# Stored weight sums of a two-layer encoder, made by HBM copies and adding transfers instead of VectorE

## The chip, the cores and the metric

The kernel runs on one core of a Trainium2 chip. The core has a matrix engine (TensorE, PE in the profile; PEld is its weight load), a vector engine (VectorE, DVE), an activation engine (ScalarE, ACT), GpSimd (POOL) and SyncE (SP), each with its own queue of instructions that it works off in order. Transfers between HBM and on-chip memory (SBUF) run on 16 DMA engines. SP, ACT and GpSimd can issue them, and only GpSimd's can add to what lies at the destination. The metric is the time of one execution in microseconds (us); lower is better. Before the change the median of three runs is 2393.16 us (2392.74 to 2401.15).

## What is computed

256 tokens of width 2048 pass two layers. Each is a norm, a token mixer (a bidirectional mLSTM in layer 0, a bidirectional HGRN2 in layer 1), a residual addition, a second norm, and a gated feed-forward part with a short convolution, again with a residual addition. A norm closes the trunk. All of it is float32. Cut to what matters here:

```python
for layer in range(DEPTH):                       # 2
    hn = rmsnorm(h, norm_mix_g[layer])
    h = h + (mlstm_mixer if layer % 2 == 0 else hgrn_mixer)(hn, ...)
    h = h + conv_glu(rmsnorm(h, norm_ffn_g[layer]), ...)
return rmsnorm(h, final_g)

def conv_glu(hn, w_up, conv_w, conv_b, w_down):  # w_up 2048 x 11008, w_down 5504 x 2048
    a, v = jnp.split(hn @ w_up, 2, axis=-1)
    c = conv_b + <width-3 convolution of a over the tokens>
    return (jax.nn.gelu(c, approximate=False) * v) @ w_down
```

Nearly all of the work is the matrix products with weights that are read from HBM once, some 440 MB.

## The kernel before

**Products.** A float32 operand is split into a rounded part and the rest (xh + xl, wh + wl), and a product is taken from three of the four parts. Weights come in pieces of 128 x 2048 (1 MB, tile raw, loaded by line 130 or, in the up-projection, line 368); ACT rounds 1024 columns to wh (line 142), VectorE subtracts to wl (line 143), TensorE multiplies (lines 330 and 334, 346, 229). A chunk is one stretch of such products with its own PSUM banks; `stream` takes the chunks of the whole program in order.

**Stages.** mLSTM until 389 us; feed-forward of layer 0: 22 up chunks (389 to 637), down products (637 to 749), 21 up chunks (749 to 982), down products (982 to 1095); HGRN until 1678; the feed-forward of layer 1 in the same four steps until the end.

**Seven products instead of eight.** In the down products two blocks of 128 rows (of both the activations and the weights) form a couple, a 2 x 2 block product. For some couples (SEVEN, 22 in a layer, in three chunks of kind "st": 8, 8 and 6) seven block products are taken instead of eight, Winograd's form. They need four sums of the couple's weight blocks B11, B22, B21, B12, called T1 to T4. These 44 couples' sums depend on weights alone, and the kernel keeps them in an HBM buffer, tscr. `split_squares` loads them later as if they were weights (T<-tscr, raw<-tscr).

**Who makes the sums.** The generator `prepare`, once for each half of a layer's feed-forward: it loads a couple's 1 MB into two tiles pwh and pwl (two loads of 512 KB, SP's queue, line 368), makes four VectorE subtractions of 128 x 512 (line 598), and stores both tiles to tscr (line 601, SP's queue). It does so while the up chunks run.

**What sets the order.** The program is written as one stream of TensorE work; other work is given to `side` as generators that yield an estimated delay, and `side.tick` advances them. The tile framework (`schedule_with_timeline_sim=True`) then reorders the instructions of each engine by what they depend on and by its own estimate of durations; only instructions given to `tc.keep_in_program_order` (`pin`, `late`) keep their place. Transfers of HWDGE queues (SP, ACT) take turns on eight counters and GpSimd's on eight others; one that takes a counter waits for the transfer that used it last. Several small results go through GpSimd in the first mixer: rc (line 421), the square root of the first norm's mean square, by which all that leaves the first projection is scaled; the broadcasts Mb (line 764), which the heads' weights need; and rs (line 506), which scales a head's output y before TensorE transposes it (pz, line 821).

Of the kernel before, what the change touches and what calls it, by code (L numbers as in the profile page):

```python
# [8 lines left out]
F32 = mybir.dt.float32  # L9
# [3 lines left out]
ALU = mybir.AluOpType  # L13
PSUM = bass.MemoryType.PSUM

P = 128
T = 256
# [27 lines left out]
MORE = 2  # L45
MIX = 5
LEAD = 48
TEMP = 3
GATES = 4 * AH
SEVEN = (1, 2, 3, 4, 6, 7, 8, 9), (1, 2, 4, 5, 7, 8)  # L50
# [10 lines left out]
def trunk_kernel(ctx, tc, xT, x_d, fg_d, pp_d, cst_d, w_gate, w_first, w_aq, w_ak, w_av, w_ao, w_aout, w_ao2,  # L61
# [467 lines left out]
    def token_sums(mp, i, a, b, S, last=None):  # L529

        m = 384 if last else 512
        sx = mp.tile([P, 2 * m], F32R, tag=f"sx{i}", name="sx")
        for i, (x, y, op) in enumerate(((a[:, P:T], b[:, P:T], ALU.add), (a[:, P:T], a[:, 0:P], ALU.subtract),
                                        (S[:, 0:P], a[:, 0:P], ALU.subtract), (b[:, 0:P], S[:, 2 * P:3 * P], ALU.subtract))):
            dve.tensor_tensor(S[:, i * P:(i + 1) * P], x, y, op)
        act.copy(sx[:, 0:m], S[:, 0:m])
        dve.tensor_tensor(sx[:, m:2 * m], S[:, 0:m], sx[:, 0:m].bitcast(F32), ALU.subtract)
        if last:
            act.copy(last[0], S[:, m:512])
            dve.tensor_tensor(last[1], S[:, m:512], last[0].bitcast(F32), ALU.subtract)  # L540
        return [(sx[:, i * P:(i + 1) * P], sx[:, m + i * P:m + (i + 1) * P]) for i in range(m // P)] + ([last] if last else [])

    def pair(src, nk, c0, x, sums, norm, seven):

        def part(t, c):
            o = 512 * (c0 + c)
            return hm[:, t, o:o + 512]

        def mid(ps):
# [6 lines left out]
            dve.tensor_tensor(part(0, 1), part(0, 1), u, ALU.add)  # L556
            dve.tensor_tensor(part(1, 1), part(1, 1), P5, ALU.add)
            dve.tensor_tensor(u, u, P7, ALU.add)  # L558
            pool.tensor_tensor(part(1, 0), part(1, 0), u, ALU.add)  # L559
            pool.tensor_tensor(part(1, 1), part(1, 1), u, ALU.add)  # L560

        def done(ps):
            for i in range(4):
# [12 lines left out]
        ch.stored, ch.waits, ch.pool = {}, None, None  # L576
        return ch

    def prepare(mp, todo, period, finished):

        loaded = []

        def load(i):
            if i < len(todo):
                n = ("wh", "wl")[i % 2]
                r = [mp.tile([P, 1024], F32, tag=n, bufs=MORE, name=f"p{n}") for _ in range(2)]
                for j in range(2):
                    late(r[j], todo[i][0][:, j * 1024:(j + 1) * 1024])
                loaded.append(r)

        yield 18.0
        load(0)
        for i, (_, dst) in enumerate(todo):
            yield period / 2
            load(i + 1)
            B11, B22, B21, B12 = (loaded[i][j // 2][:, j % 2 * 512:(j % 2 + 1) * 512] for j in range(4))
            for x, y, out in ((B12, B22, B22), (B12, B11, B12), (B11, B22, B11), (B21, B11, B21)):
                dve.tensor_tensor(out, x, y, ALU.subtract)  # L598
# [515 lines left out]
    def ffn(layer, norm, nxt):  # L1114
        stack = ExitStack()
        box = dict(n=(2 * len(SEVEN[0]) + len(SEVEN[1])) * layer)
        chunks, pairs = [], []

        def begin():
            box["mp"] = stack.enter_context(tc.tile_pool(name="ff", bufs=1))  # L1120
# [36 lines left out]
            return go  # L1157

        for part, (f0, nf) in enumerate(((0, FA), (FA, FB))):
            GT, SX, todo, finished = [], {}, [], []  # L1160

            def prep(todo=todo, finished=finished, nf=nf):
                if not pairs[0].pool:
                    begin()
                side.push(prepare(box["mp"], todo, (nf * 10.4 - 26.0) / len(todo), finished))

            for i in range(nf):
                chunks.append(Chunk("fm", w_up[layer, f0 + i], KT, norm.x, done_up(f0 + i, i, GT, SX, SEVEN[part]),
                                    prep if i == 0 else None,
                                    swap=(2,) if part and i == 0 else (3,) if f0 + i == 1 else (), paced=True))  # L1170
            def two(src, c0, norm, seven, GT=GT, SX=SX, nf=nf, todo=todo, finished=finished):
                ch = pair(src, nf, c0, lambda k: GT[k], lambda u: SX[u], norm, seven)
                for u in seven:
                    ch.stored[u] = tscr[box["n"]]
                    todo.append((src[:, 2048 * u:2048 * (u + 1)], tscr[box["n"]]))
                    box["n"] += 1
                ch.waits, ch.pool = finished, None
                pairs.append(ch)
                return ch

# [18 lines left out]
    n0, n1, n2, n3 = Norm("mix_g", 0), Norm("ffn_g", 0), Norm("mix_g", KT), Norm("ffn_g", KT)  # L1199
    nf = FinalNorm()  # L1200
    chunks = mlstm(n0, n1)
    c, close0 = ffn(0, n1, n2)
    chunks += c
    c = hgrn(n2, n3)
    b = c[0].before
# [2 lines left out]
        close0()  # L1208
        b()
    c[0].before = swap  # L1210
    chunks += c
    c, close1 = ffn(1, n3, nf)
    chunks += c
    stream(chunks)
    close1()

# [98 lines left out]
```

## Time and profile before

| | before |
|---|---|
| runs, median of 3 | 2393.16 us |
| span of the profiled execution | 2388.1 us |
| TensorE busy | 2371.3 us, 99% |
| VectorE busy | 1939.6 us, 81% |
| ScalarE busy | 1352.4 us, 57% |
| GpSimd busy | 189.7 us, 8% |
| moved by DMA | 578.15 MB, 242 GB/s mean |
| mean DMA share, mixers / first up chunks of a layer | 0.50 to 0.67 / 0.89 |

The runs' times are measured around the execution; the span is from the first to the last instruction of one profiled execution and lies 5 us below the median. TensorE's matmuls are pipelined, so that their recorded lengths overlap: a matmul of 512 columns has a record of 0.39 us, while four follow one another in 1.07 us. The DMA share is the mean busy share of the 16 DMA engines. An engine's idle time only costs something where another waits for it, so the list of who waited for whom stands above the busy shares.

### The profile page before, as it was taken

How to read it: one execution, taken by the hardware profiler on the slowest of the kernel's cores; microseconds unless marked ns; L12 is line 12 of the kernel's file. 1: busy time of each engine (PE TensorE's matmuls, PEld its weight loads, DVE VectorE, ACT ScalarE, POOL GpSimd, SP SyncE). 2: the span in 40 equal slices, each digit the busy share in tenths (PEclk: the TensorE clock that was granted, in tenths of full speed). 3: DMA queues.
4: the chain of work that ended last, by engine and by line, in shares of the span. 5: the costliest groups of instructions: out<-in, count | busy, mean ns of one | idle time of the engine just before them, and what ended most of it. 6: DMA issues, size and time to landing. Idle time of an engine off the chain costs nothing.

```text
span 2388.1 us, 38126 instructions
## 1 busy us (share of the span) xinstructions
PE 2371.3 (99%) x14596; PEld 2027.1 (85%) x14596; DVE 1939.6 (81%) x3167; ACT 1352.4 (57%) x2141; POOL 189.7 (8%) x240
## 2 busy tenths in 40 slices
PE   9999999999999999999999999999999999999998
PEld 7888888888788888888888888888888878888887
DVE  7766687888888888767888989889788888888874
ACT  7655455555565555655555555556555566455563
POOL 0100000000000000001222222220000000000000
PEclk9999999999999999999999999999999999999999
DMA  8654546998987777755544554545798998777774
GB/s 301 201 183 163 185 184 226 324 322 323 330 340 277 271 247 242 277 190 182 177 162 175 177 175 164 175 173 190 277 324 326 333 359 310 265 244 249 246 273 143
DMA packets 105703, 578.15 MB, mean 242 GB/s; under 512 B 11936, under 2 KB 12448, under 8 KB 58672
## 3 DMA queue, kind: packets, MB, share of 16 engines
q1 hardware_dynamic: 103824, 571.71, 67.5%
q0 software_dynamic: 1120, 3.21, 0.7%
q8 instruction: 114, 1.87, 0.3%
q10 hardware_dynamic: 576, 0.79, 0.1%
q14 instruction: 69, 0.57, 0.1%
HBM read 527.37 MB, written 48.30 MB: 241 GB/s over the span
## 4 chain that ended last, share of the span: by engine, by line
PE 90%; DMA 6%; DVE 3%; issue 1%; ACT 0%; SPq 0%; POOLq 0%; POOL 0%; DVEq 0%; ACTq 0%
PE mm L330 32%; PE mm L346 23%; PE mm L334 16%; PE pc L229 10%; PE mm L229 5%; DMA pwl<-in_w_d 2%; DVE wl L143 1%; DMA T<-tscr 1%; DMA pwh<-in_w_d 1%; PE pn L793 1%; PE py L1051 1%; DMA tscr<-pwl 1%; PE pd L1001 0%; PE pz L407 0%; PE pa L1001 0%
## 5 line engine op out<-in xcount | busy, mean ns | idle before, releaser
L330 PE MATMUL mm<-xt,wh 128*128 128x512 f32 x3776 | 1314.0, 394 | 0.0
L143 DVE TENSOR_TENSOR wl<-raw,wh 128x1024 fp32r<-128x1024 f32 (+1 forms) x846 | 1033.4, 1227 | 268.7 <-ACT wh L142 265.3
L142 ACT CAST wh<-raw 128x1024 fp32r<-128x1024 f32 (+1 forms) x846 | 874.4, 1040 | 567.1 <-PE mm L330 265.6
L334 PE MATMUL mm<-xt,wl 128*128 128x256 f32 x3776 | 1046.6, 278 | 1.1 <-DVE wl L143 1.1
L330 PEld LDWEIGHTS mm<-xt,wh 128*128 128x128 f32 x3776 | 706.2, 188 | 159.3
L334 PEld LDWEIGHTS mm<-xt,wl 128*128 128x128 f32 x3776 | 709.5, 188 | 6.5 <-DVE wl L143 2.0
L346 PE MATMUL mm<-wh,xt 128*128 128x512 f32 x1024 | 320.6, 391 | 1.8 <-ACT xt L352 1.3
L346 PEld LDWEIGHTS mm<-wh,xt 128*128 128x128 f32 x1024 | 191.5, 188 | 42.0 <-ACT xt L352 1.7
L346 PE MATMUL mm<-wl,xt 128*128 128x512 f32 x512 | 198.2, 391 | 0.0
L229 PE MATMUL pc<-wh,g 128*128 128x512 f32 x576 | 195.1, 390 | 0.3 <-ACT wh L142 0.2
L229 PEld LDWEIGHTS pc<-wh,g 128*128 128x128 f32 x576 | 108.0, 188 | 24.8 <-ACT wh L142 2.0
L229 PE MATMUL pc<-wl,g 128*128 128x512 f32 x288 | 112.3, 390 | 0.9 <-DVE wl L143 0.9
L346 PEld LDWEIGHTS mm<-wl,xt 128*128 128x128 f32 x512 | 96.2, 188 | 18.9
L143 DVE TENSOR_TENSOR wl<-T,wh 128x1024 fp32r<-128x1024 f32 (+1 forms) x100 | 93.8, 951 | 21.7 <-ACT wh L142 21.3
L229 PE MATMUL mm<-wh,sx 128*128 128x512 f32 x300 | 107.1, 391 | 2.8 <-ACT wh L142 2.8
L142 ACT CAST wh<-T 128x1024 fp32r<-128x1024 f32 (+1 forms) x100 | 82.3, 835 | 45.7 <-PE pc L229 23.3
L559 POOL TENSOR_TENSOR hm<-hm,u 128x512 f32<-128x512 f32 x8 | 11.2, 1399 | 1151.6 <-DVE u L558 1151.6
L1138 ACT ACTIVATE avc<-avc,pp 128x256 f32<-128x256 f32 x86 | 51.6, 600 | 87.7 <-DVE avc L1136 87.7
L346 PE MATMUL mm<-wh,g 128*128 128x512 f32 x308 | 96.5, 392 | 0.0
L1133 ACT COPY avc<-mm 128x256 f32<-128x256 f32 x172 | 63.7, 371 | 51.4 <-PE mm L334 50.9
L598 DVE TENSOR_TENSOR pwl<-pwl 128x512 f32<-128x512 f32 x88 | 60.2, 684 | 27.9 <-DMA pwl<-in_w_d 27.9
L598 DVE TENSOR_TENSOR pwh<-pwh 128x512 f32<-128x512 f32 x88 | 60.2, 684 | 27.8 <-DMA pwh<-in_w_d 21.6
(256 smaller groups left out, 2504.3 us busy)
## 6 DMA issues: line engine op xcount, KB each, us to landing
raw<-in_w_up SPq DMA_DIRECT2D x172, 1024.0 KB, 6.1
raw<-in_w_bq SPq DMA_DIRECT2D x48, 1024.0 KB, 4.9
raw<-in_w_d SPq DMA_DIRECT2D x40, 1024.0 KB, 5.2
raw<-in_w_d SPq DMA_DIRECT2D x44, 768.0 KB, 6.7
T<-tscr SPq DMA_DIRECT2D x44, 768.0 KB, 8.0
raw<-in_w_ao SPq DMA_DIRECT2D x24, 1024.0 KB, 4.6
pwh<-in_w_d SPq DMA_DIRECT2D x44, 512.0 KB, 8.1
pwl<-in_w_d SPq DMA_DIRECT2D x44, 512.0 KB, 7.7
```

The costliest lines, as they stand in the source:

```text
L142: pin(act.copy(wh[:, :m], r))
L143: pin(dve.tensor_tensor(wl[:, :m], r, wh[:, :m].bitcast(F32), ALU.subtract))
L229: pe.matmul(ps, a, b, start=id(ps) not in begun, stop=stop and i == 2)
L330: pe.matmul(ps[f], wh[:, c:c + P], x, start=k + kk == 0, stop=False)
L334: pe.matmul(ps[f][:, 0:T], wl[:, c:c + P], x[:, 0:T], start=False, stop=k + kk == ch.nk - 1)
L346: pe.matmul(ps[t], x[:, a + t * P:a + (t + 1) * P], w[:, c], start=st and i == 0, stop=sp and i == 2)
L559: pool.tensor_tensor(part(1, 0), part(1, 0), u, ALU.add)
L598: dve.tensor_tensor(out, x, y, ALU.subtract)
L793: pe.matmul(pn[:, 0:258], w, v, start=(i == 0), stop=(i == len(parts) - 1))
L1051: pe.matmul(py[:, c], AT[:, s if s == t else 2 + s], V[:, s, j * P:(j + 1) * P], start=(s == 0), stop=(s == 1))
L1133: act.copy(z, p[:, T:2 * T])
L1138: act.activation(c, a, AF.Identity, bias=col("conv_b", layer * FT + f), scale=cw[1])
```

## The change

`prepare` makes the sums without SBUF and without VectorE. For each of the 44 couples it copies the couple's four blocks from the weights to tscr (1 MB, HBM to HBM, ACT's queue), and then adds in place by four GpSimd transfers of 128 x 512 each: B12 onto the copy of B22 (T3), B11 onto the copy of B12 (T1), T3 onto the copy of B11 (T2), T2 onto the copy of B21 (T4). An adding transfer can't subtract, so the sums become additions, and the signs move to the activations' sums and to the results' combination. `prepare` of a layer now starts before the third chunk of layer 0's mixer and the second chunk of layer 1's, with an estimated 24 us for each couple; before, it started with the first up chunk of each half. Neither the copies nor the adding transfers are pinned to the program's order.

```diff
+PERIOD = 24.0
...
             for x, y, out in ((B12, B22, T3), (B12, B11, B12), (B22, B12, T2), (B21, T2, T4)):
-                dve.tensor_tensor(out, x, y, ALU.subtract)
+                dve.tensor_tensor(out, x, y, ALU.add)
...
-    def prepare(mp, todo, period, finished):
-        loaded = []
-        def load(i):
-            if i < len(todo):
-                n = ("wh", "wl")[i % 2]
-                r = [mp.tile([P, 1024], F32, tag=n, bufs=MORE, name=f"p{n}") for _ in range(2)]
-                for j in range(2):
-                    late(r[j], todo[i][0][:, j * 1024:(j + 1) * 1024])
-                loaded.append(r)
-        yield 18.0
-        load(0)
-        for i, (_, dst) in enumerate(todo):
-            yield period / 2
-            load(i + 1)
-            B11, B22, B21, B12 = (loaded[i][j // 2][:, j % 2 * 512:(j % 2 + 1) * 512] for j in range(4))
-            for x, y, out in ((B12, B22, B22), (B12, B11, B12), (B11, B22, B11), (B21, B11, B21)):
-                dve.tensor_tensor(out, x, y, ALU.subtract)
-                yield period / 8
-            for j in range(2):
-                nc.sync.dma_start(dst[:, j * 1024:(j + 1) * 1024], loaded[i][j])
-        finished.append(True)
+    def prepare(todo, period):
+        for src, dst, last in todo:
+            nc.scalar.dma_start(dst, src)
+            yield period / 4
+            T2, T3, T4, T1 = (dst[:, j * 512:(j + 1) * 512] for j in range(4))
+            B11, B22, B21, B12 = (src[:, j * 512:(j + 1) * 512] for j in range(4))
+            pool.dma_start(T3, B12, accum_op=ALU.add)
+            pool.dma_start(T1, B11, accum_op=ALU.add)
+            yield period / 4
+            pool.dma_start(T2, T3, accum_op=ALU.add)
+            yield period / 4
+            pool.dma_start(T4, T2, accum_op=ALU.add)
+            if last is not None:
+                last.append(True)
+            yield period / 4
...
-        return chunks, stack.close
+        return chunks, stack.close, lambda: side.push(prepare(todo, PERIOD))
...
-    c, close0 = ffn(0, n1, n2)
+    c, close0, chunks[2].before = ffn(0, n1, n2)
...
-    c, close1 = ffn(1, n3, nf)
-    chunks += c
+    d, close1, c[1].before = ffn(1, n3, nf)
+    chunks += c + d
```

Where the instructions stand after the framework's reordering, on the two engines that issue the new transfers. First GpSimd's queue in the first mixer, before the change (from the casts of a constant to the second broadcasts):

```order
L691 CAST Vh<-pad 128x2x2 x2
L691 CAST Vl<-pad 128x2x2 x2
L421 ISA
L421 TENSOR_TENSOR rc<-rc,mhalf 128x2
L717 MEMSET B 64x256
L733 DMA mscr<-M 64x256
L764 DMA Mb<-mscr 128x256 x12
L506 TENSOR_TENSOR rs<-rs,mhalf 128x2 x2
L764 DMA Mb<-mscr 128x256 x4
```

With the change, around rc (lines 587, 588, 590 and 592 are the four adding transfers, T3, T1, T2 and T4; rc is now line 422, B line 710):

```order
L588 DMA tscr<-in_w_d 128x512
L422 ISA
L422 TENSOR_TENSOR rc<-rc,mhalf 128x2
L587 DMA tscr<-in_w_d 128x512
L588 DMA tscr<-in_w_d 128x512
L590 DMA tscr<-tscr 128x512
L587 DMA tscr<-in_w_d 128x512
L588 DMA tscr<-in_w_d 128x512
L710 MEMSET B 64x256
```

Sixty-six adding transfers stand ahead of rc, where before none did. And further down, around the last adding transfers (the broadcasts Mb are now line 757, rs line 507):

```order
L590 DMA tscr<-tscr 128x512 x8
L592 DMA tscr<-tscr 128x512
L590 DMA tscr<-tscr 128x512 x2
L592 DMA tscr<-tscr 128x512 x22
L757 DMA Mb<-mscr 128x256 x2
L592 DMA tscr<-tscr 128x512 x2
L757 DMA Mb<-mscr 128x256 x2
L592 DMA tscr<-tscr 128x512 x10
L507 TENSOR_TENSOR rs<-rs,mhalf 128x2 x2
L757 DMA Mb<-mscr 128x256 x8
L507 TENSOR_TENSOR rs<-rs,mhalf 128x2 x6
```

All 176 adding transfers, of both layers, stand ahead of the first two rs. On TensorE's queue the first transposes pz that use them stand behind 280 matmuls of 512 columns (before the change behind 329). Last, ACT's queue in the first projection, with the counters that an instruction waits for (raw_180 is the fifth of its 16 weight tiles; DMAHW are the counters of SP's and ACT's transfers; wh is line 143 now, the copies are line 583):

```order
L583 DMA tscr<-in_w_d 128x2048 [waits DMAHW1_49]
L583 DMA tscr<-in_w_d 128x2048 [waits DMAHW3_49]
L143 CAST wh<-raw_180 128x512 [waits DMAHW4_49,DVE_49,PE_49]
L353 ACTIVATE xt_270<-gx 128x256 [waits DMAHW2_49]
L583 DMA tscr<-in_w_d 128x2048 [waits DMAHW5_49]
L583 DMA tscr<-in_w_d 128x2048 [waits DMAHW7_49]
L583 DMA tscr<-in_w_d 128x2048 [waits DMAHW1_49]
L143 CAST wh<-raw_181 128x512 [waits DMAHW6_49,DVE_49,PE_49]
```

Before, casts and activations alone alternate there. Now all 44 copies stand among the first 16 casts, 42 of them ahead of that of raw_184.

More of the change, by code (lines that the diff above doesn't have):

```diff
@@ L532, in token_sums @@
         sx = mp.tile([P, 2 * m], F32R, tag=f"sx{i}", name="sx")
-        for i, (x, y, op) in enumerate(((a[:, P:T], b[:, P:T], ALU.add), (a[:, P:T], a[:, 0:P], ALU.subtract),
-                                        (S[:, 0:P], a[:, 0:P], ALU.subtract), (b[:, 0:P], S[:, 2 * P:3 * P], ALU.subtract))):
+        for i, (x, y, op) in enumerate(((a[:, P:T], b[:, P:T], ALU.subtract), (a[:, P:T], a[:, 0:P], ALU.subtract),
+                                        (S[:, 0:P], a[:, 0:P], ALU.subtract), (b[:, 0:P], S[:, 2 * P:3 * P], ALU.add))):
             dve.tensor_tensor(S[:, i * P:(i + 1) * P], x, y, op)
@@ L555, in mid @@
             dve.tensor_tensor(part(0, 1), part(0, 1), P5, ALU.add)
-            dve.tensor_tensor(part(0, 1), part(0, 1), u, ALU.add)
+            dve.tensor_tensor(part(0, 1), part(0, 1), u, ALU.subtract)
             dve.tensor_tensor(part(1, 1), part(1, 1), P5, ALU.add)
-            dve.tensor_tensor(u, u, P7, ALU.add)
+            dve.tensor_tensor(u, u, P7, ALU.subtract)
             pool.tensor_tensor(part(1, 0), part(1, 0), u, ALU.add)
-            pool.tensor_tensor(part(1, 1), part(1, 1), u, ALU.add)
+            pool.tensor_tensor(part(1, 1), part(1, 1), u, ALU.subtract)
         def done(ps):
@@ L1116, in ffn @@
         box = dict(n=(2 * len(SEVEN[0]) + len(SEVEN[1])) * layer)
-        chunks, pairs = [], []
+        chunks, pairs, todo = [], [], []
         def begin():
@@ L1159, in ffn, with two @@
         for part, (f0, nf) in enumerate(((0, FA), (FA, FB))):
[L1160 to L1165, printed above, removed]
+            GT, SX = [], {}
             for i in range(nf):
                 chunks.append(Chunk("fm", w_up[layer, f0 + i], KT, norm.x, done_up(f0 + i, i, GT, SX, SEVEN[part]),
-                                    prep if i == 0 else None,
+                                    begin if part == i == 0 else None,
                                     swap=(2,) if part and i == 0 else (3,) if f0 + i == 1 else (), paced=True))
-            def two(src, c0, norm, seven, GT=GT, SX=SX, nf=nf, todo=todo, finished=finished):
+            def two(src, c0, norm, seven, GT=GT, SX=SX, nf=nf):
                 ch = pair(src, nf, c0, lambda k: GT[k], lambda u: SX[u], norm, seven)
+                ch.waits = []
                 for u in seven:
                     ch.stored[u] = tscr[box["n"]]
-                    todo.append((src[:, 2048 * u:2048 * (u + 1)], tscr[box["n"]]))
+                    todo.append((src[:, 2048 * u:2048 * (u + 1)], tscr[box["n"]], ch.waits if u == seven[-1] else None))
                     box["n"] += 1
-                ch.waits, ch.pool = finished, None
                 pairs.append(ch)
```

1 line of the change is left out of this document (removed).

## The prediction

> **What bounds the kernel now.** First the page: busy times, queues, chain.
>
> ```profile
> span 2388.1 us, 38126 instructions
> PE 2371.3 (99%) x14596; PEld 2027.1 (85%) x14596; DVE 1939.6 (81%) x3167; ACT 1352.4 (57%) x2141; POOL 189.7 (8%) x240
> q1 hardware_dynamic: 103824, 571.71, 67.5%
> q0 software_dynamic: 1120, 3.21, 0.7%
> PE 90%; DMA 6%; DVE 3%; issue 1%; ACT 0%; SPq 0%; POOLq 0%; POOL 0%; DVEq 0%; ACTq 0%
> ```
>
> TensorE is idle for 2388.1 - 2371.3 = 16.8 us. The chain gives DMA 6%, but it follows the last releaser backwards, through loads that TensorE did not stand still for. So I asked next for the waits of PE itself, and then for busy times by stage (columns of the second: stretch, its length, busy time of PE, PEld, DVE, ACT, POOL, granted clock, DMA share, GB/s).
>
> ```profile
> PE mm L229 <- ACT wh L142: 2.8, 2, 1.5
> PE mm L346 <- ACT xt L352: 1.3, 1, 1.3
> ...
> PE mm L334 <- DVE wl L143: 1.1, 2, 0.9
> ```
>
> ```profile
> 0.00:36.00 36.00, 33.43 (x337) 27.00 (x338) 22.41 (x37) 27.23 (x54) 1.39 (x12) 1.00 0.98 367
> 36.00:95.00 59.00, 59.00 (x309) 50.10 (x308) 48.79 (x105) 39.96 (x67) 8.72 (x16) 1.00 0.67 210
> 95.00:389.00 294.00, 294.00 (x1481) 249.16 (x1480) 211.10 (x350) 164.89 (x261) 10.75 (x14) 1.00 0.52 179
> 389.00:637.00 248.00, 246.91 (x1422) 215.19 (x1421) 212.08 (x353) 135.97 (x217) 0.70 (x1) 1.00 0.89 316
> 637.00:749.00 112.00, 109.62 (x481) 89.38 (x480) 96.59 (x107) 72.23 (x86) 4.35 (x2) 1.00 0.88 329
> 1923.00:2036.00 113.00, 111.10 (x484) 89.69 (x483) 98.45 (x109) 74.97 (x90) 3.53 (x2) 1.00 0.89 330
> ```
>
> The reader is to see two things. TensorE waits for nearly nothing at a full clock, so it is the bound in every stage, also where the DMA engines are 0.89 busy and the sums are made. And the feed-forward stages that the change relieves hold 1.1 + 2.4 + 1.9 = 5.4 us of TensorE idle time in all (length less busy time of the last three rows; the other feed-forward stretches show none, or the kernel's tail).
>
> The other thing to read is GpSimd's queue in the first 100 us, since the change puts 176 transfers on it, and the TensorE instruction that needs its later results. In order of time (start, length, instruction, idle before and its releaser):
>
> ```profile
> 36.75 0.71 POOL L421 TENSOR_TENSOR rc<-rc,mhalf 128x2 f32<-128x2 f32 x1 [4.32 <-DVE rc L420]
> 63.50 2.18 POOL L764 DMA_DIRECT2D Mb<-mscr  x4 [1.68 <-DMA mscr<-M]
> 94.52 0.72 POOL L506 TENSOR_TENSOR rs<-rs,mhalf 128x2 f32<-128x2 f32 x1 [7.98 <-DVE rs L505]
> ```
>
> ```profile
> 99.47 0.60 PE L821 MATMUL pz<-cst,y 128*128 128x128 f32 x4
> ```
>
> rc (the first norm's factor) at 36.75 us scales everything that leaves the first projection. rs at 94.52 us scales the first two heads' outputs, which TensorE transposes from 99.47 us on.
>
> **The change, part by part.** Removed: the subtractions, the loads of their operands and the stores.
>
> ```profile
> L598 DVE TENSOR_TENSOR pwl<-pwl 128x512 f32<-128x512 f32 x88 | 60.2, 684 | 27.9 <-DMA pwl<-in_w_d 27.9
> L598 DVE TENSOR_TENSOR pwh<-pwh 128x512 f32<-128x512 f32 x88 | 60.2, 684 | 27.8 <-DMA pwh<-in_w_d 21.6
> tscr<-pwl SPq DMA_DIRECT2D x44, 512.0 KB, 6.8
> ```
>
> That is 176 x 0.684 = 120 us of VectorE, and 88 loads and 88 stores of 512 KB on SP. TensorE's work covers all of it, so its removal brings at most the 5.4 us above; I take 5. If that cover were gone, VectorE's 120 us would count, but no row of TensorE's waits names L598. The changed signs (additions for subtractions in the matmul's other sums and in the eight results) keep engine, shape and count, and cost nothing.
>
> Added: 44 copies of 1024 KB on ACT's queue (44 x 1.049 = 46.1 MB) and 176 adding transfers of 256 KB on GpSimd's (again 46.1 MB written). The instruction order shown with the change says where: not spread at 24 us each from the mixers on, but all of both layers at the program's start. Three things stand behind them:
> - ACT's casts of the first projection's weights. raw_184's cast stands behind 42 copies, each of which waits for the last transfer on its counter.
> - rc, behind 66 adds. Before, it ran at 36.75 us.
> - rs of the first two heads, behind all 176. TensorE's queue is in order, so from the first pz on everything waits: the projections, and the weights' loads, since raw buffers come free only as TensorE goes on.
>
> The last decides. With T the time at which GpSimd gets past the last add, rs follows at T and pz about 2 us later (rs 0.7, a scaling, a transpose's start). The work of TensorE ahead of pz is 99.5 us less 49 matmuls of 512 columns, which the new order puts behind it. Those run at 0.227 us:
>
> ```profile
> 17.44 0.87 PEld L346 LDWEIGHTS mm<-wh,xt 128*128 128x128 f32 x4
> 17.66 1.07 PE L346 MATMUL mm<-wh,xt 128*128 128x512 f32 x4
> 18.80 0.87 PEld L346 LDWEIGHTS mm<-wh,xt 128*128 128x128 f32 x4
> 19.02 1.07 PE L346 MATMUL mm<-wh,xt 128*128 128x512 f32 x4
> ```
>
> (1.36 us from one group of six, two of them wl, to the next.) So 99.5 - 11.1 = 88.4 us, and the delay is T + 2 - 88. The stalls at the casts and at rc lie inside it: rc needs a third of the adds, and only 50 us of TensorE's work lies between it and pz.
>
> T is a sum of what the 16 DMA engines have to move by then. No row shows a transfer from HBM to HBM or one that adds, so I price them by q1 and q0 of the page. q1 took 0.675 x 2388.1 / 571.71 = 2.82 us of all engines for a MB; q0, GpSimd's own queue, 0.007 x 2388.1 / 3.21 = 5.2 us.
> - Copies, 46.1 MB: 130 us if a MB counts once as in q1, 260 us if reading and writing HBM both count. I take the middle, 195.
> - Adds, 46.1 MB of results, each from two reads: lower bound 46.1 x 2.82 = 130 us (as if the second read were free), upper bound three passes at q0's price, 138 x 5.2 = 720 us. Two reads cost 260 us at q1's price and 480 at q0's; I take the middle, 370, since their 2 KB rows lie nearer to q0's packets and their size nearer to q1's transfers.
> - Loads up to pz: 367 GB/s x 36 us + 210 GB/s x 52 us = 24.2 MB, 68 us.
> - The last eight adds need not have landed: 8/176 of 370, -17.
>
> T = 195 + 370 + 68 - 17 = 616 us; delay 616 + 2 - 88 = 530 us; less 5, plus 525. The span becomes 2388.1 + 525 = 2913 us. The runs' median lies 5 us above the profiled span (2393.16 against 2388.1), so **2918 us**. With all lower bounds T is 130 + 130 + 68 - 6 = 322 and the time 2624 us; with all upper ones 260 + 720 + 68 - 33 = 1015 and 3317 us.
>
> Issuing is no larger term: GpSimd needs 0.55 us for a transfer, 97 us for 176, beside their landing. Nor is the limit of eight in flight (each add waits for the eighth before it), while one lands as fast as these, 176 x 6.0 / 8 = 132 us:
>
> ```profile
> L764 POOL DMA_DIRECT2D Mb<-mscr x16: 536/546/585, 63.5 to 146.3; - x16
> Mb<-mscr POOLq DMA_DIRECT2D x16, 128.0 KB, 6.0
> ```
>
> Two sentences of the Trainium skill bear on the sum. "DMA: Bandwidth & Descriptors", section "Issuing engines are not separate DMA queues", says that transfers issued from several engines share the same 16 DMA engines and save only issue time; by that rule the terms add, as in T, and no run here shows the opposite (three queues side by side would make T the adds' 353 us alone, and the time about 2655 us). The same page, section "Latency and other measured facts", gives 207 to 214 GB/s for copies from HBM to HBM, by which, as an estimate, the copies would take 220 us instead of 195 and the time would be 2943 us; no run here shows one yet.
>
> **The rivals.**
> - *Cheap transfers*: a byte counts once on the engines, or the three queues overlap. For it: 4 KB and 8 KB rows of q1 run at up to 367 GB/s in the first row above. Against it: an add must read two operands. About 2624 us; all of 2500 to 2750.
> - *Dear adds*: small rows that read, add and write back to HBM go nearly one at a time. Then 176 x 6.0 us (the landing of a 128 KB transfer of this queue) = 1056 us, with copies and loads beside it, is T: 2388 + 1056 + 2 - 88 - 5 + 5 = 3358 us. For it: q0's bytes cost nearly twice those of q1. Against it: 256 KB should not need 6 us of 16 engines' time.
> - *The waits are hidden* (the other side): GpSimd's queue keeps up with its consumers, rc at 36.75 us finds 66 adds issued, and only the feed-forward's relief is left: 2388.1 - 5 + 5 = 2388 us, not slower. For that one add would have to land each 36.75 / 66 = 0.56 us from the start, which is its issue time, and 30 copies in 36 us, 870 GB/s where the page's best stretch above moved 367. It decides from there: each further 0.1 us for an add moves rs by 18 us. The rows nearly exclude it.
> - *The change doesn't do what it says*: its words put the sums into the mixers' stretches at DMA shares of 0.5. If the order on the chip were so, 92 MB over some 900 us of mixers would fit into the free half, and the time would also be about 2388. The order is what runs, so I give this nothing of its own.
>
> **How the numbers follow.** The forecast's stall with 2750 to 3100 us: 0.47. Cheap transfers: 0.25. Dear adds, above 3100: 0.24. Hidden: 0.04, half faster and half the same (0.5%, 12 us, is about what a measurement of this kernel can tell from no change). So slower 0.96. The range goes from a little under the sum of the lower bounds to a little over the one-at-a-time case: 2600 to 3400 us.
>
> **What would show it.** In the changed profile TensorE's idle time should be near 530 us, nearly all in the first 650 us, put down to ACT's casts, to rc and then to rs or y behind GpSimd; the last add should be issued near 616 us, and the DMA share be 0.9 or more until then. From about 100 us of work on, every stage should last as long as before, within 3 us, at a granted clock of 1.00. If the copies end near 130 us, or an add lands on average in 0.8 us of the time left, the cheap rival holds; at 5 us or more the dear one. I am wrong altogether if rc runs before 50 us, if TensorE's idle time lies in the feed-forward stages, or if the DMA share is low while GpSimd waits, since then latency and not bytes sets T.

## The result, and the profile after

The changed kernel takes 2746.52 us (median of 4 runs, 2745.42 to 2746.98); the kernel before took 2394.77 us beside it (4 runs, 2392.74 to 2401.15). The ratio is 1.147, with a 95% interval of 1.145 to 1.148. The profiled execution grew from 2388.1 to 2745.2 us, by 357.1 us. The page of the changed kernel, as far as it answers to that of before (the three rows of digits are its 40 slices of 68.6 us):

```profile
span 2745.2 us, 37875 instructions
PE 2394.0 (87%) x14596; PEld 2042.2 (74%) x14596; DVE 1863.6 (68%) x2991; ACT 1350.7 (49%) x2141; POOL 334.0 (12%) x416
PE   2113514999999999999999999999999999999998
...
PEclk5556756999999999999999999999999999999999
DMA  9999998554555579655755545454555558855574
...
PE 82%; issue 0%; DVE 0%; ACT 0%; POOLq 0%; POOL 0%
```

TensorE is idle for 2745.2 - 2394.0 = 351.2 us, nearly all of it in the first seven slices, in which the DMA engines are full. The chain of waits attributes only 82% to TensorE and next to nothing to any other engine: it does not name the loss. The waits of TensorE do:

```profile
PE mm L347 <- ACT xt L353: 171.7, 8, 38.7
PE pn L786 <- ACT Wh L777: 66.1, 2, 65.0
PE pz L814 <- DVE y L809: 46.6, 1, 46.6
PE pr L432 <- DVE dg L429: 36.8, 1, 36.8
PE pt L731 <- DVE C L720: 10.2, 1, 10.2
```

These are, in this order, activations and casts on ACT behind the copies, the heads' weights that need Mb, the heads' outputs that need rs, what follows rc, and the gates' C, which needs the buffer B that GpSimd clears behind the adds. GpSimd's timeline shows the three instructions the prediction spoke of (start, length, idle before):

```profile
263.29 1.35 POOL L422 TENSOR_TENSOR rc<-rc,mhalf 128x2 f32<-128x2 f32 x1
...
366.44 0.60 POOL L757 DMA_DIRECT2D Mb<-mscr  x1 [0.47 <-DMA tscr<-tscr]
...
437.63 4.18 POOL L592 DMA_DIRECT2D tscr<-tscr  x5 [0.46 <-DMA tscr<-tscr]
441.44 1.79 POOL L507 TENSOR_TENSOR rs<-rs,mhalf 128x2 f32<-128x2 f32 x2
```

```profile
443.24 1.94 PE L814 MATMUL pz<-cst,y 128*128 128x128 f32 x8 [46.60 <-DVE y L809]
```

rc came at 263 us instead of 37, the first Mb at 366 instead of 64, rs at 441.4 instead of 94.5, right behind the last adding transfers. TensorE's first pz followed 1.8 us later. The same in stretches (columns as in the prediction: length, busy times of PE, PEld, DVE, ACT, POOL, clock, DMA share, GB/s):

```profile
0.00:50.00 50.00, 13.76 (x204) 10.36 (x204) 4.36 (x8) 5.31 (x9) 11.59 (x21) 0.64 0.98 304
50.00:100.00 50.00, 5.85 (x12) 3.64 (x12) 2.18 (x4) 2.06 (x4) 7.32 (x9) 0.53 1.03 300
...
200.00:250.00 50.00, 25.04 (x138) 19.61 (x138) 13.84 (x25) 17.29 (x37) 13.85 (x21) 0.77 1.02 260
...
400.00:443.00 43.00, 0.00 (x0) 0.00 (x0) 0.39 (x1) 0.00 (x0) 27.04 (x35) 0.50 1.10 194
443.00:453.00 10.00, 7.20 (x20) 5.16 (x21) 8.44 (x15) 6.84 (x9) 0.23 (x1) 0.50 0.81 168
453.00:463.00 10.00, 10.00 (x44) 8.24 (x43) 4.31 (x8) 3.59 (x4) 2.29 (x4) 0.96 0.85 295
...
500.00:1000.00 500.00, 500.00 (x2692) 430.18 (x2691) 374.40 (x608) 283.13 (x451) 10.50 (x13) 1.00 0.55 186
```

From 500 us on TensorE is as busy as before at a full clock. What the DMA engines moved until rs, by queue (packets, MB, share of the 16 engines in the first 441 us; q0 is GpSimd's, q10 the copies, q1 the loads):

```profile
q0 software_dynamic: 24909, 45.73, 62.0%
q10 hardware_dynamic: 6624, 46.41, 28.4%
q1 hardware_dynamic: 6336, 21.61, 14.2%
```

That is 273 us for the adds, 125 us for the copies and 63 us for the loads, 461 us of engine time in 441 us (the shares of concurrent packets add up to a little over one).

### The profile page after: what moved, and what is told of

It is laid out like the page before. It is cut to its first block, busy times and chain, and to the rows that moved or that the text cites. A ratio compares the mean times of both kernels' runs of the same rounds, so it can differ in the third digit from the quotient of the medians.

```text
span 2745.2 us, 37875 instructions
## 1 busy us (share of the span) xinstructions
PE 2394.0 (87%) x14596; PEld 2042.2 (74%) x14596; DVE 1863.6 (68%) x2991; ACT 1350.7 (49%) x2141; POOL 334.0 (12%) x416
## 4 chain that ended last, share of the span: by engine, by line
PE 82%; issue 0%; DVE 0%; ACT 0%; POOLq 0%; POOL 0%
PE mm L331 31%; PE mm L347 17%; PE mm L335 16%; PE pc L230 10%; PE mm L230 5%; PE py L1044 1%; PE pn L786 0%; PE pd L994 0%; PE pz L408 0%; PE pa L994 0%; PE S L772 0%; PE pa L1018 0%; PE pz L1065 0%; PE pa L1019 0%; PE pz L814 0%
## 5 line engine op out<-in xcount | busy, mean ns | idle before, releaser
L347 PE MATMUL mm<-wh,xt 128*128 128x512 f32 x1024 | 333.1, 403 | 174.9 <-ACT xt L353 171.7
L347 PEld LDWEIGHTS mm<-wh,xt 128*128 128x128 f32 x1024 | 197.1, 194 | 220.6 <-ACT xt L353 177.1
L1127 DVE TENSOR_TENSOR avc<-mm,avc 128x256 f32<-128x256 f32 x172 | 72.4, 421 | 20.5 <-ACT avc L1126 20.4
L786 PE MATMUL pn<-Vh,Wh 128*128 128x258 f32 x48 | 14.4, 306 | 66.1 <-ACT Wh L777 66.1
L986 DVE COPY kq<-QK 128x256 f32<-128x256 f32 x224 | 70.2, 339 | 0.0
```

Source lines behind the costliest of these rows:

```text
L347: pe.matmul(ps[t], x[:, a + t * P:a + (t + 1) * P], w[:, c], start=st and i == 0, stop=sp and i == 2)
L786: pe.matmul(pn[:, 0:258], w, v, start=(i == 0), stop=(i == len(parts) - 1))
L986: dve.tensor_copy(m[:, j].rearrange("k (m p j) -> k m p j", p=2, j=h), blocks(z, h, 0, T))
L1127: dve.tensor_tensor(z, p[:, 0:T], z, ALU.add)
```

## The experiments

The question after the result is which part of the 352 us belongs to what: to copies, to adds, to their place in the queues. The rival reading is that the order hardly matters, and that 92 MB of transfers cost what they cost. All ratios are against the kernel before on the same chip. The framework reorders each edited program anew, so other instructions can move too; the waits are read beside the times for that reason.

**No sums at all: the floor.** Neither copies nor adds; the couples' blocks are loaded from the weights instead of the sums, so the seven-product couples take wrong operands, at the same sizes.

```diff
-            nc.scalar.dma_start(dst, src)
...
-            pool.dma_start(T3, B12, accum_op=ALU.add)
-            pool.dma_start(T1, B11, accum_op=ALU.add)
...
-                    ch.stored[u] = tscr[box["n"]]
+                    ch.stored[u] = src[:, 2048 * u:2048 * (u + 1)]
```

> Neither copies nor adds; the stored couples' blocks are loaded from the weights themselves instead of tscr, with the same loads (this leaves out the sums, so the seven products are not those of the reference). It is the floor for any way to make the sums. Theory (TensorE is the bound, and the sums cost it only the 5.4 us of idle time in the feed-forward stages): 2385 to 2391 us. Rival (VectorE's 120 us and the DMA share of 0.89 slow TensorE's pace without showing as waits): under 2375 us.

Measured: 2380.59 us (5 runs), ratio 0.9946 (0.9933 to 0.9958), 4 us below the theory and above the rival. Span 2379.3 us, TensorE busy 2367.7 us: 3.6 us less than before, which the theory put at nothing. All that the sums cost the kernel before is 13 us by the medians and 8.8 us by the spans. No way of making them can bring more than that.

**Copies alone.** The four adds are left out, so that the stored blocks are not the sums; the copies stand where the change put them.

```diff
-            pool.dma_start(T3, B12, accum_op=ALU.add)
-            pool.dma_start(T1, B11, accum_op=ALU.add)
...
-            pool.dma_start(T2, T3, accum_op=ALU.add)
...
-            pool.dma_start(T4, T2, accum_op=ALU.add)
```

> The change without its adds: the 44 copies stay at the start, 38 of them ahead of the cast of raw_184 (this leaves out the sums' additions). Theory (the terms add on the DMA engines, and the copies took 26.1% of 480 us = 125 us of all engines): ACT's casts wait until some 36 copies have landed, which with the first loads takes about 130 us, less the 20 us at which that cast stood before: about 2500 us (2480 to 2530). Rival (the adds alone hold the kernel, the copies go beside the first projection): under 2420 us.

Measured: 2539.27 us (2 runs), ratio 1.061. TensorE's waits, and the copies' queue in the first 230 us:

```profile
PE mm L347 <- ACT xt L353: 119.1, 9, 25.2
```

```profile
q10 hardware_dynamic: 6624, 46.41, 55.3%
```

The copies alone cost 145 us, 9 us above the end of the theory's range, and the wait is at one place: ACT's casts and activations behind copies that wait for their counters. Their bytes take 0.553 x 230 = 127 us of all engines, 2.7 us for a MB, as in the changed kernel.

**Eight copies, all adds; and the same adds four times as wide.**

```diff
-        for src, dst, last in todo:
-            nc.scalar.dma_start(dst, src)
+        for src, dst, last, fill in todo:
+            if fill:
+                nc.scalar.dma_start(dst, src)
...
-                    ch.stored[u] = tscr[box["n"]]
+                    ch.stored[u] = tscr[box["n"] % 8]
```

(fill holds for the first eight couples), and in the second kernel, in place of the four adds of 128 x 512:

```diff
+            pool.dma_start(dst, src, accum_op=ALU.add)
```

which adds the couple's whole 128 x 2048.

> The changed kernel, not pinned, with 8 copies in place of 44; all 176 adds stay, but those of all couples pile up on eight buffers, so the sums are wrong. Theory (the DMA engines' time is the sum of copies and adds, at 2.7 us for a MB copied and 6 us for a MB added, with loads beside them): 8 copies 23 us, 83 adds that now stand ahead of the first rs 83 x 0.262 MB x 6 = 130 us, loads 70 us: T near 225 us, the delay some 135 us, 2500 to 2550 us. Rival (the copies only fill gaps, adds set the pace at the 5 us each that they showed while copies flowed): 83 x 5 = 415 us, delay 330 us, about 2720 us.

> As the kernel with 8 copies, but one adding transfer of 1 MB (rows of 8 KB) in place of four of 256 KB (rows of 2 KB), so that the bytes of results are the same; the sums are wrong. 22 of these adds stand ahead of the first rs. Theory: an added MB costs the DMA engines two to three passes whatever its rows are: 22 x 1.05 MB x 6 = 138 us, and the time is within 15 us of that kernel's. Rival: the price is one of rows (2 KB descriptors): with rows four times as long an added MB falls to some 3 us, and T and the time are 50 to 70 us less.

Measured: 2540.78 us (ratio 1.061, 1.059 to 1.063) with 256 KB adds, 2551.28 us (1.065, 1.063 to 1.067) with 1 MB adds. GpSimd's queue in the first 250 us, of the first kernel and of the second:

```profile
q0 software_dynamic: 13280, 24.71, 58.3%
```

```profile
q0 software_dynamic: 3776, 24.71, 48.6%
```

Both theories' ranges hold (2500 to 2550 us, and within 15 us of it). The same 24.71 MB take 0.583 x 250 / 24.71 = 5.9 us for a MB in rows of 2 KB, and 4.9 us in rows of 8 KB. In the first kernel the sum of engine times named T well: the first rs ran at 218.5 us (forecast 225). That the whole delay of 146 us lies so near the 135 forecast is in part luck. At its output projection this kernel is only 107.6 us late (its first matmul pc<-wh,ya at 431.1 us, before at 323.5). The rest is lost later, most of it in HGRN, where TensorE is idle for 33 us between 1000 and 1700 us: the adds of layer 1 reuse the eight buffers, and the first of them is issued only at 824 us, when a load of layer 0's sums from these buffers has landed (T<-tscr). Wider rows make an added MB cheaper by a sixth, not by half, so the length of the rows is the smaller part of the price. The second kernel's time did not follow that gain; it is 10 us longer, and its stall lies elsewhere (63.6 us behind ACT's activations, 21.2 at the heads' weights), so its time does not test the price, only the share does.

**The program's order kept, whole and for the adds alone.**

```diff
-            nc.scalar.dma_start(dst, src)
+            pin(nc.scalar.dma_start(dst, src))
...
-            pool.dma_start(T3, B12, accum_op=ALU.add)
+            pin(pool.dma_start(T3, B12, accum_op=ALU.add))
```

and so for the other three adds; in the second kernel the copy is left as the change has it.

> The change with its copies and adds kept in the program's order on their queues, so that they run from the third chunk of each mixer on, one couple per some 24 us, and nothing of the first projection stands behind them. Theory (the 352 us come from where the transfers stand, ahead of ACT's casts and of rc, Mb and rs on GpSimd's queue): the stall is gone and the time is 2385 to 2400 us, with TensorE's idle time under 30 us. Rival (the price lies in the transfers wherever they stand: 92 MB more work for the DMA engines in the mixers, and adds that hold GpSimd's queue in order there): over 2420 us, with TensorE waiting in the HGRN stage.

> The change with only the adds kept in program order; the copies stay at the start as in the run without adds. Theory (ACT's queue and GpSimd's queue each hold the start on their own): as without adds within 15 us, about 2500 us. Rival (GpSimd's queue is the one that holds the kernel, ACT's stall would be made up): under 2420 us.

Measured: 2504.48 us (5 runs), ratio 1.047 (1.044 to 1.049), and 2650.8 us (2 runs), ratio 1.108. Keeping the order takes away 241 of the 352 us, so the order is what most of the loss hangs on. But 110 us stay: the first time lies in the rival's range (over 2420 us), though not mainly in HGRN, where the rival put it, and the second lies in neither range. And with the copies left at the start, both losses add: 145 + 111 = 256, measured 2650.8 - 2393.9 = 257. The two stalls lie at different places and do not hide each other. Where the 110 us lie in the wholly kept order, by TensorE's waits, by two stretches and by GpSimd's waits:

```profile
PE pc L230 <- ACT wh L143: 23.7, 3, 20.0
PE pr L432 <- DVE dg L429: 23.5, 2, 18.8
PE pz L408 <- DVE hm L566: 19.3, 2, 14.5
```

```profile
300.00:400.00 100.00, 74.19 (x313) 59.43 (x312) 54.88 (x88) 39.01 (x59) 13.04 (x16) 0.86 0.93 285
400.00:500.00 100.00, 76.42 (x392) 65.00 (x391) 53.16 (x78) 42.04 (x69) 23.25 (x27) 0.88 0.87 199
...
1700.00:1800.00 100.00, 79.39 (x363) 65.57 (x362) 65.34 (x98) 46.13 (x71) 20.29 (x24) 0.91 0.91 249
```

```profile
POOL tscr L590 <- DMA tscr<-in_w_d: 265.1, 44, 17.9
POOL tscr L592 <- DMA tscr<-tscr: 254.4, 42, 12.3
```

Both mixers' ends, where the output projection, the residual addition hm and the second norm's rc follow one another. GpSimd stands for over 500 us at adds whose source has not landed, and hm and rc are GpSimd's work. So my next theory was that these waits are the cause.

**A lag between each add and its source.**

```diff
+        for i in range(n + 3):
+            if i < n:
+                pin(nc.scalar.dma_start(todo[i][1], todo[i][0]))
             yield period / 4
+            if 0 <= i - 1 < n:
...
+                pin(pool.dma_start(T3, B12, accum_op=ALU.add))
+                pin(pool.dma_start(T1, B11, accum_op=ALU.add))
             yield period / 4
+            if 0 <= i - 2 < n:
...
+                pin(pool.dma_start(T2, T3, accum_op=ALU.add))
             yield period / 4
+            if 0 <= i - 3 < n:
...
+                pin(pool.dma_start(T4, T2, accum_op=ALU.add))
```

> The change with its transfers kept in the program's order, as in the experiment that took 2504 us, but no adding transfer follows its source at once: at each step of 24 us the copy of couple i is issued, T3 and T1 of couple i - 1, T2 of couple i - 2 and T4 of couple i - 3. The computation is complete. Theory: in that experiment the 110 us were lost because GpSimd's queue stood at adds whose copy or preceding add had not landed (265 and 254 us of waits), with hm and rc of the second norms behind them. With a step between, the sources have landed, GpSimd waits for at most some 20 us in all, and the stalls of TensorE at hm, rc and pz go: 2381 to 2395 us, the lower end being the 2380.6 us of the kernel without sums. Rival: it is the transfers' bytes on the DMA engines (92 MB and more, late weights) or the issue of 176 adds that cost the 110 us, and the waits on GpSimd only show it: then 2450 to 2510 us, with TensorE waiting for casts.

Measured: 2498.91 us (5 runs), ratio 1.043 (1.041 to 1.044), in the rival's range. The theory fell: GpSimd's waits at adds dropped to 242 us (134.1, 95.0 and 12.9 in its three groups), and the time by 6 us. The stall is at the same place, and now ACT's timeline at its beginning tells what it is:

```profile
321.21 1.05 ACT L143 CAST wh<-raw 128x1024 fp32r<-128x1024 f32 x1 [1.66 <-PE mm L347]
321.23 32.60 ACTq L589 DMA_DIRECT2D tscr<-in_w_d  x12
353.88 0.63 ACT L502 ACTIVATE jk<-hm 128x512 f32<-128x512 f32 x1 [31.62 <-DMA tscr<-in_w_d]
```

Twelve copies in a row, which should stand 24 us apart, and ACT waits behind them for 32 us. GpSimd's order shows the same of the adds: 25 of layer 0's 88 stand ahead of the last head's rs, and then 34 between it and the next hm. The reason is in the program, not on the chip: the output projection's first result calls side.drain() (in the function mixed, a line that the change does not touch), and this steps every side job to its end, due or not. Since the change, the sums are a side job that is alive at that point. So "at an estimated 24 us for each couple" is not what the program's order says either.

**The sums left to their own pace.**

```diff
-                for job in list(self.jobs):
+                for job in [j for j in self.jobs if not j[2]] or list(self.jobs):
...
-            self.until(lambda: not self.jobs)
+            self.until(lambda: all(j[2] for j in self.jobs))
...
-        return chunks, stack.close, lambda: side.push(prepare(todo, PERIOD))
+        return chunks, stack.close, lambda: side.push(prepare(todo, PERIOD), True)
```

once with the lag, and once on the kept order without it.

> As the kernel with its transfers lagged by a step (2499 us), with one more edit: in the program's planner, drain and until, which the mixers' output projections call, step all other side work but leave the sums to their own pace of 24 us. The computation is complete. Before, drain had put 34 of layer 0's 88 adding transfers and ten copies in a row into the output projection of the first mixer, and 27 into the second's; now 10 and 7 lie there. Theory: those bunches made the two stalls (300 to 480 us and 1700 to 1790 us, some 90 us of TensorE's time together); without them only the HGRN's 15 to 20 us of small waits stay: 2395 to 2415 us. Rival: 176 adds beside the mixers' own loads and GpSimd's own work are too much at any pace, and the loss spreads without shrinking by more than a third: 2450 to 2490 us.

> As the change kept in the program's order (2504 us: each add right behind its source), with the same edit of drain and until: the sums keep their own pace, no bunches. The computation is complete. It tells whether the lag between an add and its source matters once the bunches are gone. Theory: little, since without bunches a copy lands within 12 us and GpSimd's waits of some 10 us an add fall where nobody needs it, except in HGRN, where its own work for each head comes behind them: 2395 to 2430 us, within 15 us of the lagged kernel. Rival: GpSimd's waits are the cost as such: 2440 to 2490 us, while the lagged one is near 2400.

Measured: 2417.31 us (6 runs), ratio 1.0094 (1.0077 to 1.0112), and 2428.7 us (6 runs), ratio 1.0141 (1.0115 to 1.0166). The bunches were the cause of most of the 110 us: from 2498.91 and 2504.48 us, 82 and 76 us are gone with this one edit. The lagged kernel ends 2 us above what I gave it; the lag is worth 11 us, which fits "within 15". The idle time that is left lies largely in HGRN, where GpSimd has work of its own for every head (of the lagged kernel; the stretch of before shows 99.70 here):

```profile
1200.00:1300.00 100.00, 94.84 (x841) 80.08 (x840) 88.91 (x188) 49.76 (x95) 36.26 (x47) 0.97 0.77 229
```

Over 1100 to 1700 us TensorE is idle for 12.9 us with the lag and 21.0 us without (0.3 us before): that is most of the 11 us between the two.

**The sums moved to stages with room.** First six couples of layer 1 left in HGRN, ten moved to layer 0's second stretch of up chunks and six to layer 1's first; then none in HGRN and none meant for a down product.

```diff
-    c, close0, chunks[2].before = ffn(0, n1, n2)
+    chunks[2].before = lambda: sums0(0, 22)
...
-    d, close1, c[1].before = ffn(1, n3, nf)
+    up0.before = lambda: sums1(0, 10)
+    c[1].before = lambda: sums1(10, 16, 60.0)
+    def up1():
+        begin1()
+        sums1(16, 22)
```

(sums0 and sums1 start the sums of a layer's couples from the first number to the second; up0 is layer 0's second stretch of up chunks, c[1] a chunk of HGRN, up1 runs ahead of layer 1's first up chunks.) The second kernel has 22 couples of layer 0 at 21 us and two of layer 1 behind them, then `sums1(2, 9)` at up0, `sums1(9, 16, 22.0)` in up1 and `sums1(16, 22)` at layer 1's second up chunks.

> As the kernel with lag and own pace, with layer 1's couples moved to where GpSimd and the DMA engines have room: ten couples in layer 0's second stretch of up chunks, six at 60 us each in HGRN, six in layer 1's first stretch of up chunks. The computation is complete. Theory: the remaining loss of HGRN falls to a third and the feed-forward's relief of 13 us (the kernel without sums took 2380.6 us) shows: 2383 to 2395 us, at or a little below the kernel before. Rival: adding transfers beside the up chunks' loads make weights late there, as the DMA share before of 0.89 hints: 2400 to 2430 us.

> As the kernel with spread sums (2408 us), with none left in HGRN or in the down products: layer 0's couples at 21 us each from the first mixer on, two of layer 1's after them in the same stretch of up chunks, seven in layer 0's second stretch of up chunks, seven in layer 1's first and six in its second. The computation is complete. Theory: of the 27 us that the spread kernel lay above the kernel without sums (2380.6), HGRN held some 8, and the sums that reached into the down products some 12, since there the loads are at a share of 0.89 already; these go, and the start, the first mixer's output projection and the up chunks stay: 2386 to 2398 us, about the kernel before. Rival: the bytes cost wherever they go, since a share of 0.9 in the up chunks makes weights late too: 2400 to 2415 us.

Measured: 2407.82 us (6 runs), ratio 1.0056 (1.0038 to 1.0074), and 2398.44 us (12 runs), ratio 1.0022 (1.0009 to 1.0034). The first missed its theory (2395 at most) and fell into the rival's range, but not for the rival's reason: from 400 to 600 us and from 800 to 1000 us, in the up chunks, TensorE stays 100% busy at DMA shares of 0.88 to 0.94. Most of its idle time between 400 and 1100 us lies in the down products (6.3 us from 600 to 800 us, 4.8 us from 1000 to 1100 us, where 3.5 us and none were idle before), into which adds had run over. The second ended 0.4 us above the upper end of its theory. Of it:

```profile
1200.00:1300.00 100.00, 99.88 (x888) 85.64 (x888) 93.33 (x198) 54.47 (x103) 29.69 (x39) 1.00 0.50 169
```

```profile
PE mm L230 <- ACT wh L143: 6.2, 2, 4.3
PE pc L230 <- ACT wh L143: 5.6, 2, 5.2
```

HGRN is whole again. Its profiled span is 20.2 us above the floor's: 24.2 - 11.6 = 12.6 us more of TensorE's idle time (mostly these two groups of waits for casts, in the first mixer's output projection and in the first down product) and 2375.3 - 2367.7 = 7.6 us more of busy time. This is the best of the versions with sums by transfers: within 0.5% of the kernel before, and by its interval a trace slower. None beat the kernel before. Whether those two waits can be planned away as well was not tried; the floor leaves 0.5% to be had.

## Why the prediction was right or wrong

**The order on the queues decides, and rs ends the stall: right.** rs ran at 441.44 us behind the last adds, pz at 443.24, 1.8 us later (forecast 2). Against the 88.4 us of TensorE's work ahead of pz that is a delay of 354.8 us; the span grew by 357.1. The remaining 2.3 us are what the program behind pz takes more: 2745.2 - 443.2 = 2302.0 us, against 2388.1 - 99.5 + 11.1 = 2299.7. That they are so few is luck, as two larger differences cancel. The starts of TensorE's matmuls in the output projection (ya) and in the down products (g) show them, first and last, before and after:

```profile
L229 PE MATMUL pc<-wh,ya x92: 389/389/389, 323.5 to 364.7; 128*128 128x512 f32 x92
L229 PE MATMUL pc<-wh,g x576: 387/389/507, 637.2 to 2322.0; 128*128 128x512 f32 x192
L230 PE MATMUL pc<-wh,ya x92: 389/389/389, 689.4 to 730.7; 128*128 128x512 f32 x92
L230 PE MATMUL pc<-wh,g x576: 389/389/397, 1001.0 to 2678.8; 128*128 128x512 f32 x192
```

At the output projection the changed kernel is 689.4 - 323.5 = 365.9 us late, 11 us more than at pz. From pz to 500 us TensorE is idle for 4.8 us, and its granted clock is 0.88 in the mean over 52 us of work; as an estimate from these, 4.8 + 0.12 x 52 = 11.0 us. At the last down product it is 2678.8 - 2322.0 = 356.8 us late, so the stages from there on win back 9.1 us. The step "delay = T + 2 - 88" is right in kind, but it leaves out these 11 us, and the first mixer behind pz did not stay within the 3 us named.

**T was too large: 616 us against 441.** The failing step is the pricing, "I take the middle", in two terms.
- Copies: 195 forecast, 125 measured. A MB counts once, as in the loads' queue; 130 was my lower bound. That is 70 us.
- Adds: 370 - 17 = 353 forecast, 273 measured, 6.0 us for a MB of result. That is 80 us. "Two reads at q1's price" (260 for all of them) was nearest, and I had moved from it towards q0's price; one pass at q0's price (240) is about as near, so what the 6.0 us are made of is not shown. One reason that I gave for moving, the rows of 2 KB, is not borne out for loads by the profile before. In its first 36 us, for which I spoke of rows of 4 and 8 KB, 16 tiles have rows of 2 KB; q1 moved 12.89 MB there in 5127 packets, 2.5 KB each in the mean, in 0.949 x 36 us, or 2.65 us for a MB.
- Loads: 68 forecast, 63 measured, 5 us (24.2 MB should read 24.1). And the shares of concurrent queues come to 461 us in 441: 20 us less than a plain sum.

70 + 80 + 5 + 20 = 175 = 616 - 441. The rest of the way from 2918 to 2746 us are the 11 us above, 4 us more of relief than forecast, and the distance from the span to the median, 5 us before and 1.3 us here: 2918 - 175 + 11 - 4 - 4 = 2746.

That the terms add follows from what "DMA: Bandwidth & Descriptors" in the Trainium skill says in "Issuing engines are not separate DMA queues", that all queues share the same 16 engines; the trace agrees, to those 20 us, and T in the kernel with eight copies does too. The 207 to 214 GB/s that I took from the Trainium skill, "DMA: Bandwidth & Descriptors", "Latency and other measured facts", stand there for copies whose rows lie 512 KiB or more apart. They were no price for these copies, whose source rows lie 172 KiB apart at most by the arrays' shapes: 46.41 MB in 125 us of the 16 engines' time is 371 GB/s.

**The cases.** The measured time lies 3.5 us below the border that I drew between the stalled case (2750 to 3100) and cheap transfers (2500 to 2750), so by the time alone it is the cheap rival's, to which I gave 0.25. By that rival's two tests it is not quite cheap either: the copies' last issue is at 199.6 us and not near 130, and the 129 adds from 236 us to 441 take 1.6 us each, not 0.8. A MB counted once for the copies and about twice for the adds. Both cases have the same mechanism, and the time lies between their two sums, 2918 and 2624. That it lies inside 2600 to 3400 owes much to the width of that range. Dear adds, 5 us and more for each, and the hidden waits were wrong. GpSimd takes 0.81 us to issue an adding transfer and not the 0.55 of a broadcast, which changes nothing while its landing is slower:

```profile
L587 POOL DMA_DIRECT2D tscr<-in_w_d x44: 807/812/1502, 11.6 to 324.0; - x44
L592 POOL DMA_DIRECT2D tscr<-tscr x44: 802/813/1448, 236.3 to 440.9; - x44
```

**Relief: 5 us forecast, 9.1 measured.** The changed kernel has it too, as the starts above show; the kernel without sums has 8.8 us by the spans, 13 by the medians. The idle time of the three feed-forward stretches, which I counted, did go: behind 500 us no wait of TensorE for a cast is left. What I put at nothing is its busy time, 3.6 us less without the sums.

**"Doesn't do what it says": wrong as it was argued.** I wrote that with the sums spread over the mixers the time would be about 2388, since 92 MB fit into the DMA engines' free half. The bytes do fit into the program: the last plan, with all the bytes, reaches 2398. But the program's order costs 110 us. In the order in which the edits took them away, 76 us are drain's bunches in the output projections; 11 us are adds that stand in GpSimd's queue until their source has landed, most of it in HGRN; 19 us went when sums left HGRN and the down products; and 4 us are left. I priced a resource's mean and left out queues.

**Signs in the profile.** TensorE's idle time is 351 us instead of 530, 342 of it before 500 us; the DMA share stays at 0.98 to 1.10 until the last add; casts, Mb, rc and rs are named. That the largest single wait (171.7 us) belongs to ACT and not to rs is no contradiction: it lies inside T, as the copies alone (145 us) and the whole (352 us) show.

## What to carry to other kernels

A transfer that depends on nothing is free to go to the head of its queue, and an in-order queue then makes every later instruction of that engine wait for it; read the order of the built program first, find the last instruction behind the bunch that TensorE needs, and add up engine time until there. Free bandwidth as a mean tells only that a plan could exist: what a moved transfer costs is set by what stands behind it on its issuing engine, and by planner calls such as drain that ignore its pace. Before moving work, run the kernel without it: here the whole prize was 9 to 13 us.

## What the runs showed of the hardware

- A copy from HBM to HBM took the DMA engines 2.7 us for a MB in three kernels (46.41 MB in 125 and 127 us, 8.66 MB in 0.094 x 250 = 23.5 us), no more than a load.
- An adding transfer from HBM to HBM took 5.9 to 6.0 us for a MB of result in rows of 2 KB, 4.9 us in rows of 8 KB.
- The granted clock fell to 0.50 to 0.53 while TensorE stood, and the first work after the stall paid for it: from 443 to 453 us 0.50, from then on 0.96. A matmul of 512 columns took about 0.42 us there instead of 0.23 (from one start to the next below, before and after the return). TensorE's busy time rose by 22.7 us in all, most of it ahead of pz. The Trainium skill tells of this in "TensorE: Matmul & The Clock Gate", "Part 1: The HAM clock gate (the "warmup" mystery)": after at least one idle window of some 3.4 us the clock is halved, and at least one busy window of about that length restores it. The trace agrees: about half while TensorE stood, and a return after some 6 us of work (from 447.7 us on).

```profile
449.56 0.63 PE L347 MATMUL mm<-wh,xt 128*128 128x512 f32 x1
449.98 0.63 PE L347 MATMUL mm<-wl,xt 128*128 128x512 f32 x1
...
454.09 0.39 PE L347 MATMUL mm<-wl,xt 128*128 128x512 f32 x1
454.32 0.39 PE L347 MATMUL mm<-wh,xt 128*128 128x512 f32 x1
```
